# A one-core hybrid layer (gated DeltaNet and differential attention): load order and passes of the first projection, planned times of the gates' transpositions, weights of attention's order

## The chip, the cores and the metric

The kernel runs on one core of one Trainium2 chip. The metric is device microseconds of one execution; lower is better. The kernel before was run three times: median 1941.17 us (1939.21 to 1942.13).

## What is computed

One layer over 1024 latent tokens with a prefix of 256 context tokens, model width 1024. Modulation comes from c, normalisation and one wide projection feed two branches, and both are gated, merged and projected:

```python
shift, scale, gate = jnp.split(jax.nn.silu(c) @ w_ada + b_ada, 3, axis=-1)
h = rms_norm(x) * (1.0 + scale[:, None]) + shift[:, None]      # context: the same with c_ctx
qkv_a, z_a, a_raw, b_raw, q_b, k_b, v_b, z_b, gates = split_cols(h @ w_in)
o_a = gdn_bidirectional(...)   # 8 heads: short conv on q, k, v, then a chunked gated delta rule both ways
o_b = diff_attend(q, k, v, lam)  # 8 heads: softmax(s0) - lam * softmax(s1), times v
y_a = rms_norm(o_a) * silu(z_a);  y_b = rms_norm(o_b) * (1 - lambda_init) * silu(z_b)
merged = g_a * (y_a @ w_oa) + g_b * (y_b @ w_ob)
return x + gate * (merged @ w_out)
```

Wide products are computed in three passes from operands split in a high and a low part (high·high, low·high, high·low), so each product of the reference is three matmuls.

## The kernel before

**How the order comes about.** The program is written as streams: Python generators, each of which yields one operation after the other as an engine, an estimated duration, the tokens (planned ends) that it waits for, and the code that issues it. A planner, at build time, decides in which order the operations go to each engine. `turn_flow` (front and attention) finds the earliest planned start of all streams' next operations and, among those on that engine that could start within TOL = 0.02 us of it, takes the stream with the smallest bias; `flow` (convolution, DeltaNet and filling projections) takes the smallest sum of start and bias, and the projections that fill TensorE's waits there have FB0 added to their start. `later(t, us)` only moves a planned end: it delays nothing on the chip, but may put other operations first. At run time every engine goes through its list in order, and waits by semaphores.

**Stages** (times from the trace). The front, up to about 75 us: `loads` issues all transfers on SP's queue (L265 is the line of each of these DMAs); `modulation` multiplies a padded c with w_ada in four parts u, each in two halves of 1 MB (TensorE mp<-wa,pad, sixteen matmuls of 256 columns; the sums are copied to mrow by VectorE, L354, and ScalarE, L352); `rms` squares each block of 128 tokens of x on ScalarE (L381), takes the power -0.5 on POOL and scales on VectorE (L385); `turns` transposes scaled x (pt); `turned` makes h, its high part on ScalarE (L402), the whole on VectorE (L405) and the low part (L408) on VectorE for even k and POOL for odd k; `weights` splits the first weights of w_in (wr) in wh (ScalarE, L316) and wl (VectorE, L317). `main` is the first projection (mm<-hs,wh and mm<-hs,wl). Tokens go in groups: 0 and 1 of four latent blocks each (512 columns), 2 of the two context blocks. ORDER runs over the four units u of k pairs and the groups 0 and 1, then group 2.

The convolution stage follows (to about 430 us), in which the gates of the DeltaNet are computed once: three matmuls into one bank (gp), a copy to gcc (VectorE, L848), a difference (L849), exponentials (egl on ScalarE, L850), and ten transpositions of gcc in groups of four, four and two (trg), copied to gr (VectorE, L861). The three banks `tr0` to `tr2` go round through the list `pfree`, in which each comes with the tokens of its last readers.

Then the DeltaNet scan with filling projections (to about 1300 us; their last outputs are SiLU gates zo, ScalarE, L1039), attention (to about 1760 us), and the second half of the merge with the output projection (to the end).

**Attention** has named streams whose biases are the table ABIAS, to each of which `due` adds the index of the tile in work, so that a difference of 10 between two weights is a lead of ten tiles: scores (TensorE s<-kk,qh and s<-kk,ql), evs (VectorE takes s out of its bank, L1565), softs (the minimum, then the exponential over 1280 keys on ScalarE, L1578), scales (L1595 on ScalarE, or POOL), adds (POOL, L1602), turns (TensorE t<-ct,S, ten transpositions of one tile of weights, three banks), highs (ScalarE cast ah<-t, L1634), lows (VectorE al, L1639), att_out (TensorE v<-ah and v<-al, 30 matmuls for two tiles), outs (ScalarE's square osq, L1669, and through gateq VectorE's oT, L1676), sums (TensorE v<-ct,osq, columns of sums), norms (a power, the transposition m<-ct,bry), merge (TensorE ma<-y,wh and ma<-y,wl, the first half of the merge, which fills waits) and mouts (VectorE g, L1812, empties the merge's bank). There are 64 tiles of scores: 8 heads of 8 blocks. merge and m share one bank, pm.

Of the kernel before, what the change touches and what calls it, by code (L numbers as in the profile page):

```python
# [17 lines left out]
P = 128  # L18
D = 1024
KT = D // P  # L20
# [14 lines left out]
PE, DVE, ACT, POOL, DMA, ADMA, DV2, PL1 = range(8)  # L35
# [8 lines left out]
class Block:  # L44
# [30 lines left out]
    def flow(self, until):  # L75
# [3 lines left out]
        while not until():  # L79
# [3 lines left out]
            for s in self.streams:  # L83
# [7 lines left out]
                if s[1] is None:  # L91
                    start += self.FB0 if self.units_done < self.FT else self.FB1
                if h[0] == PE and len(h) > 4 and self.heat - self.HEAT * (start - clk[PE]) < 0:
# [144 lines left out]
    def front(self, st, early, kv0):  # L238
# [5 lines left out]
        xt, wa, raws, T = {}, {}, {}, {}  # L244
# [19 lines left out]
        def get(us, dst, src, deps=()):  # L264
            return DMA, us, list(deps), lambda: nc.sync.dma_start(dst, src)  # L265

        def loads():
            r = [(yield get(0.02, rows[0:8, :], a["c"].rearrange("o (k p) -> (o k) p", p=P))),
                 (yield get(0.02, rows[8:16, :], a["c_ctx"].rearrange("(k p) -> k p", p=P)))]
            T["rows"] = [self.later(x, -1.2) for x in r]  # L270
            for o in "xw0sy123zv":
                if o == "s":
                    r = [(yield get(0.05, rw2[0:24, :], a["b_ada"].rearrange("o (k p) -> (o k) p", p=P))),
                         (yield get(0.02, rw2[24:25, :], a["gdn_norm_w"])), (yield get(0.02, rw2[25:26, :], a["diff_norm_w"])),
                         (yield get(0.25, rw3, a["conv_w"].rearrange("o j (k p) -> (o j k) p", p=P)))]
                    T["rw"] = r
                elif o in "0123":
                    u = int(o)
                    if u == 3:
                        yield lambda: ("mm", 0) in T  # L280
                    for i in range(2):
                        if u == 2:
                            wa[u, i] = fu.tile([P, KT, W], F32, tag=f"u{i}", name="wa")
                        elif u == 1:
                            wa[u, i] = self.hc.tile([P, KT, W], F32, tag=f"s2{i}", name="wa")
                        else:
                            wa[u, i] = self.wab[0].tile([P, KT, W], F32, tag=("wh", "wl")[i], name="wa")
                        T["wa", u, i] = self.later((yield get(3.0, wa[u, i], a["w_ada"][0, :, i * D + u * W:i * D + (u + 1) * W].rearrange(
                            "(k p) n -> p k n", p=P), [T["mm", 0]] if u == 3 else ())), -1.2)
                elif o == "w":  # L290
                    for s in range(2):
                        k = slice(s * KT // 2, (s + 1) * KT // 2)
                        raws[s] = raw = self.wr.tile([P, KT // 2, W], F32, tag="wr", name="wr")
                        T["w0", s] = self.later((yield get(1.5, raw, kv0.rearrange("(k p) n -> p k n", p=P)[:, k])), -1.2)
                elif o == "v":
                    yield lambda: ("w", 1) in T and ("mm", 3) in T
                    for s in range(2):
                        k = slice(s * KT // 2, (s + 1) * KT // 2)
                        raws[s] = raw = self.wr.tile([P, KT // 2, W], F32, tag="wr", name="wr")
                        yield get(1.5, raw, self.wcols(C_VB).rearrange("(k p) n -> p k n", p=P)[:, k], [T["w", s]])  # L300
                        T["w1", s] = self.later((yield get(0.3, grw[:, k], a["w_in"][0, :, C_AB:C_AB + 32].rearrange(
                            "(k p) n -> p k n", p=P)[:, k])), -1.2)
                else:
                    for t in groups["xyz".index(o)]:
                        T["x", t] = self.later((yield get(1.5, xt[t], a["x"][0, t * P:(t + 1) * P, :] if t < NL else
                                                          a["ctx"][0, (t - NL) * P:(t - NL + 1) * P, :])), -1.2)

        def weights():
            for i, n in ((0, W), (1, W + 32)):
                yield lambda: (f"w{i}", 1) in T  # L310
                hl, ends = [self.wab[1 - i].tile([P, KT, n], F32R, tag=t, name=t) for t in ("wh", "wl")], []
                for s in range(2):
                    k = slice(s * KT // 2, (s + 1) * KT // 2)
                    for o, rw, us in ((0, raws[s], 0.256), (W, grw[:, k], 0.032))[:1 + i]:
                        c = slice(o, o + rw.shape[2])
                        t1 = yield ACT, 0.1 + 3.6 * us, [T[f"w{i}", s], T.get(("mm", 3))], lambda: nc.scalar.copy(hl[0][:, k, c], rw)  # L316
                        t2 = yield DV2, 4.7 * us, [t1], lambda: V.tensor_tensor(  # L317
                            hl[1][:, k, c], rw, hl[0][:, k, c].bitcast(F32), ALU.subtract)
                        ends += [t1, t2]
                    self.raw_t[s] = t2  # L320
                    if i == 0:
                        T["w", s] = [t1, t2]
                T["hl"] = T.get("hl", hl)
                if i:
                    self.parts_[1] = *hl, ends

# [85 lines left out]
        def main():  # L412
            pts = [self.pm.tile([P, 512], F32, tag="mm", name="mm") for _ in range(5)]
            for g, ks in ORDER:
                n = len(groups[g]) * P
                for s, k in [(s, k) for s in range(2) for k in ks]:
                    yield lambda: ("h", g, k) in T and ("w", k // 4) in T
                    th, tl, _ = self.hsel(groups[g][0])
                    pt = pts[4][:, s * W:s * W + W] if g == 2 else pts[2 * s + g]
                    for i, (wt, ht) in enumerate(((0, th), (0, tl), (1, th))):  # L420
                        e = yield PE, 0.2265 if n == 512 else 0.1195, [T["h", g, k], T["w", k // 4]], lambda: self.mm(
                            pt, T["hl"][wt][:, k, s * P:(s + 1) * P], ht[:, k, :n], k == i == 0, k == KT - 1 and i == 2)
                    if k == KT - 1:
                        self.first_[s, g] = pt, e
            self.parts_done, self.part_t[0] = 1, e

# [378 lines left out]
    def gates(self):  # L805
# [12 lines left out]
        te = yield DMA, 0.1, [], lambda: nc.sync.dma_start(ea, a["a_log"].rearrange("o d h -> o (d h)").to_broadcast([P, NS]))  # L818
        x, y, s, z, w = (big[:, i] for i in range(5))
# [5 lines left out]
        te = yield ACT, 0.2, [te], lambda: nc.scalar.activation(ea, ea, AF.Exp), AF.Exp  # L825
# [16 lines left out]
        ib, bank, gp = self.bank("gp")  # L842
# [5 lines left out]
        tg = yield DVE, 0.25, [t], lambda: V.tensor_copy(self.gcc, v(0))  # L848
        t1 = yield DVE, 0.25, [t, tg], lambda: V.tensor_tensor(z, v(NT * NS), self.gcc, ALU.subtract)  # L849
        te = yield ACT, 0.3, [t], lambda: nc.scalar.activation(self.egl, v(NT * NS), AF.Exp), AF.Exp  # L850
        self.pfree.append((ib, [t1, te]))
        td = yield ACT, 0.3, [t1], lambda: nc.scalar.activation(self.edk, z, AF.Exp), AF.Exp
        yield ACT, 0.3, [tg], lambda: nc.scalar.activation(self.eg, self.gcc, AF.Exp), AF.Exp
        gr = gs.tile([P, LT], F32, tag="gtmp", name="gr")[:NS]
        for b0 in range(0, NT, 4):
            nb = min(4, NT - b0)
            yield lambda: self.pfree
            ib, bank, pt = self.bank("trg")
            for t in range(nb):
                e = yield PE, 0.109, [self.later(tg, 3.0), bank], lambda: self.tr(pt[:NS, t * P:(t + 1) * P], self.gcc[:, b0 + t])  # L860
            e = yield DVE, 0.6, [e, td], lambda: V.tensor_copy(gr[:, b0 * P:(b0 + nb) * P], pt[:NS, :nb * P])  # L861
            self.pfree.append((ib, e))
        yield DMA, 0.2, [e], lambda: nc.sync.dma_start(self.gcd.rearrange("d h n -> (d h) n"), gr)


# [570 lines left out]
    def named(self, n, gen):  # L1436
        s = self.entry[n] = [gen, self.ABIAS.get(n, 0), None, None]
        s[2] = next(gen, None)
        self.streams.append(s)

    def due(self, n, i):

        self.entry[n][1] = self.ABIAS.get(n, 0) + self.DUE * i

# [38 lines left out]
    WB = -0.17  # L1483
    FT = 38
    LEFT = 3
    FB0 = 0.05
    FB1 = 0.36
    COLD = 0.4
    HEAT = 0.55
# [245 lines left out]
    def side_start(self):  # L1735
# [10 lines left out]
    ONACT = (1, 2, 3)  # L1746
    TOL = 0.02
    PACE = 4.48
    ABIAS = dict(rels=-0.59, softs=8.84, norms=5.82, gateq=-27.29, sums=-18.71,
                 outs=-21.73, lows=-2.4, highs=-9.33, adds=36.19, scales=31.0, evs=22.29, mouts=-3.31,  # L1750
                 att_out=1.9, turns=3.19, scores=-21.22, merge=25.46)
    KEEP = 3

    def side_values(self):
# [454 lines left out]
```

## Time and profile before

| | us |
|---|---|
| median of three runs | 1941.17 |
| the profiled execution | 1941.8 |
| its span | 1939.9 |
| VectorE busy | 1453.6 |
| ScalarE busy | 1063.6 |
| POOL busy | 679.6 |

The page of the profile gives busy times by engine, a strip of the span in slices, the chain that ended last, and groups of instructions by line. PE is TensorE, PEld its weight loads, DVE VectorE, ACT ScalarE, POOL GpSimd, SP the queue that issues most DMAs. In a row of the timeline stand start, duration, engine, line, operation, output and inputs with their sizes, and the count of instructions; in brackets the idle time of the engine just before it, and what ended that. A group's row has the same idle time summed. Matmuls overlap, so their durations are longer than their distance from start to start.

### The profile page before, as it was taken

Reading aid. Unit: us, or ns where it says so; the run is one execution under the profiler, and the core shown is the slowest. Engines: PE = TensorE matmul, PEld = TensorE weight load, DVE = VectorE, ACT = ScalarE, POOL = GpSimd, SP = SyncE. Lnnn points to the kernel's source line nnn. Section 1 sums busy time; section 2 is a strip of 40 time slices with the busy share of each in tenths; the row PEclk is TensorE's granted clock in tenths of the full one; section 3 lists DMA queues with packets and bytes.
Section 4 is the critical chain, followed back from the end, with each engine's and each line's share of the span. In section 5 each row is a group of like instructions: output and inputs, shape, how many; then the busy total and the mean of one; then the engine's idle time right before and its main releaser. Section 6 shows DMA issues by size and latency. Waiting matters only on the chain.

```text
span 1939.9 us, 37460 instructions
## 1 busy us (share of the span) xinstructions
PE 1901.0 (98%) x13807; PEld 1675.0 (86%) x13807; DVE 1453.6 (75%) x3613; ACT 1063.6 (55%) x2189; POOL 679.6 (35%) x610
## 2 busy tenths in 40 slices
PE   6999999999999999999999999999999999999999
PEld 4978888899999998888888888887997888888887
DVE  4687998957887888767864965337996979985577
ACT  4543444426233563677575655448885868883222
POOL 3200000005541342343433232326766657671203
PEclk9999999999999999999999999999999999999999
DMA  9144535574545557667686565665436474226542
GB/s 333 61 133 98 138 95 134 127 194 171 173 141 184 173 188 230 232 196 236 196 291 199 183 199 166 206 236 201 129 123 205 162 244 148 83 88 221 185 148 87
DMA packets 383038, 336.39 MB, mean 173 GB/s; under 512 B 142609, under 2 KB 323443, under 8 KB 381831
## 3 DMA queue, kind: packets, MB, share of 16 engines
q1 hardware_dynamic: 382855, 333.99, 54.9%
q8 instruction: 109, 1.79, 0.4%
q14 instruction: 74, 0.61, 0.1%
HBM read 222.14 MB, written 111.79 MB: 172 GB/s over the span
## 4 chain that ended last, share of the span: by engine, by line
PE 83%; DVE 6%; DMA 4%; ACT 3%; issue 2%; POOL 1%; SPq 1%; DVEq 0%; ACTq 0%; POOLq 0%
PE mm L56 42%; PE s L56 6%; PE v L56 5%; PE chain L56 5%; PE mb L56 5%; PE ma L56 4%; PE x L56 3%; PE t L63 3%; PE out L56 3%; PE gram L56 1%; DVE S L1565 1%; DVE ac L595 1%; PE tr L63 1%; PE pz L56 1%; PE mp L56 1%
## 5 line engine op out<-in xcount | busy, mean ns | idle before, releaser
L56 PE MATMUL mm<-hs,wh 128*128 128x512 f32 (+1 forms) x2048 | 648.2, 390 | 1.5 <-DVE hs L408 1.4
L56 PEld LDWEIGHTS mm<-hs,wh 128*128 128x128 f32 x2048 | 371.1, 189 | 58.7 <-DVE hs L408 2.0
L56 PE MATMUL mm<-hs,wl 128*128 128x512 f32 (+1 forms) x1024 | 397.3, 388 | 1.0 <-POOL wl L886 1.0
L56 PE MATMUL mm<-wh,hs 128*128 128x256 f32 (+1 forms) x1792 | 332.8, 286 | 0.2 <-ACT sq L978 0.2
L56 PEld LDWEIGHTS mm<-wh,hs 128*128 128x128 f32 x1792 | 280.8, 191 | 0.7 <-ACT sq L978 0.4
L1565 DVE TENSOR_SCALAR_CACHE_REDUCE S<-s,rsq 128x512 f32<-128x512 f32 (+1 forms) x384 | 239.6, 655 | 30.8 <-PE s L56 28.1
L56 PE MATMUL mm<-wl,hs 128*128 128x256 f32 (+1 forms) x896 | 255.7, 285 | 0.0
L1602 POOL TENSOR_TENSOR S<-S 128x1280 f32<-128x1280 f32 x64 | 189.0, 2956 | 92.2 <-ACT S L1595 91.0
L56 PEld LDWEIGHTS mm<-hs,wl 128*128 128x128 f32 x1024 | 193.7, 189 | 29.7 <-POOL wl L886 1.4
L1578 ACT ACTIVATE S<-S,mn 128x1280 f32<-128x1280 f32 x128 | 175.2, 1371 | 51.2 <-DVE mn L1577 50.7
L56 PEld LDWEIGHTS mm<-wl,hs 128*128 128x128 f32 x896 | 171.3, 191 | 0.1
L595 DVE SCALAR_TENSOR_TENSOR ac<-xc,convT,ac 128x1284 f32<-128x1284 f32 (+1 forms) x96 | 138.7, 1447 | 11.3 <-ACT ac L593 10.7
L56 PE MATMUL s<-kk,qh 128*128 128x512 f32 (+1 forms) x384 | 143.1, 373 | 1.6 <-DVE S L1565 1.4
L56 PE MATMUL s<-kk,ql 128*128 128x512 f32 (+1 forms) x384 | 133.5, 359 | 0.0
L1639 DVE TENSOR_TENSOR al<-t,ah 128x512 fp32r<-128x512 f32 (+1 forms) x192 | 106.8, 594 | 7.4 <-ACT ah L1634 6.1
L580 POOL MEMSET xc<- 128x2 f32 (+1 forms) x64 | 3.6, 100 | 299.8 <-ACT sq L629 113.6
L1160 DVE TENSOR_TENSOR ts<-ts,tmp 80x31 f32<-80x31 f32 (+15 forms) x248 | 94.0, 379 | 6.0
L1158 DVE TENSOR_TENSOR tmp<-ab,ts 80x31 f32<-80x31 f32 (+15 forms) x248 | 93.1, 375 | 6.8 <-DMA ab<-da 1.4
L1323 ACT ACTIVATE vd<-chain,edk 128x128 f32<-128x128 f32 x144 | 52.3, 371 | 78.0 <-PE chain L56 72.2
L56 PE MATMUL ma<-y,wh 128*128 128x512 f32 x256 | 93.1, 410 | 1.7 <-DVE g L1812 1.7
L1634 ACT CAST ah<-t 128x512 fp32r<-128x512 f32 (+1 forms) x192 | 88.1, 521 | 9.8 <-PE t L63 8.5
L56 PE MATMUL v<-al,vh 128*128 128x256 f32 x320 | 90.6, 283 | 0.7 <-DVE al L1639 0.7
(296 smaller groups left out, 4314.0 us busy)
## 6 DMA issues: line engine op xcount, KB each, us to landing
wr<-in_w_in_dram SPq DMA_DIRECT2D x48, 512.0 KB, 6.3
hx<-in_w_in_dram SPq DMA_DIRECT2D x64, 256.0 KB, 4.6
x<-xq SPq DMA_DIRECT2D x64, 256.0 KB, 5.0
X<-gcd SPq DMA_DIRECT2D x8, 1280.0 KB, 7.6
kd<-col SPq DMA_DIRECT2D x40, 256.0 KB, 2.2
xq<-X SPq DMA_DIRECT2D x16, 640.0 KB, 8.8
kk<-kd SPq DMA_DIRECT2D x16, 640.0 KB, 6.1
kq<-gkq SPq DMA_DIRECT2D x8, 1152.0 KB
```

The costliest lines, as they stand in the source:

```text
L56: self.nc.tensor.matmul(out, lhsT, rhs, start=start, stop=stop)
L63: self.nc.tensor.transpose(out, src, self.ident[:src.shape[0], :src.shape[0]])
L580: x["e"].append((yield PL1, 0.1, [old], lambda: nc.gpsimd.memset(xc[:, a:b], 0.0)))
L595: t = yield DV2, 1.21e-3 * wd, [t], lambda: nc.vector.scalar_tensor_tensor(ac[:, :wd], xc[:, j:j + wd], self.convw(j, x["ct"]), ac[:, :wd] ...
L1158: t = yield DV2, n * w / 960.0 + 0.08, [t if j else self.later(t, 2.5), t1], lambda: V.tensor_tensor(tv, ab[:, j + 1:, j:j + 1].to_broadca ...
L1160: t = yield DV2, n * w / 960.0 + 0.08, [t, t1], lambda: V.tensor_tensor(ts[:, j + 1:, :w], ts[:, j + 1:, :w], tv, ALU.subtract)
L1323: td = yield ACT, 0.251, [t], lambda: nc.scalar.activation(vd, pc[:, 1], AF.Copy, scale=self.edk[:, c, g:g + 1])
L1565: e = yield DVE, 0.675 if m == 512 else 0.408, [e, self.sfree[c].get(n - 4 + c)], lambda: self.nc.vector.tensor_scalar(x["S"][c][:, o:o + ...
L1578: x["x"].append((yield ACT, 1.36, [e], lambda: nc.scalar.activation(S, S, AF.Exp, bias=x["mn"][:, c:c + 1], scale=-1.0, accum_out=w["l0"][ ...
L1602: e = yield POOL, 2.9, [e], lambda: self.nc.gpsimd.tensor_tensor(S0, S0, S1, ALU.add)
L1634: e = yield ACT, 0.48 if nb == 4 else 0.27, [t, y["old", k]], lambda: self.nc.scalar.copy(y["ah", k][:, :, q], pv)
L1639: t = yield DVE, 0.603 if k < 2 else 0.322, [e, y["old", k]], lambda: self.nc.vector.tensor_tensor(y["al", k][:, :, q], pv, y["ah", k][:, ...
```

## The change

It has four parts. In `loads`, the order of groups goes from `xw0sy123zv` to `0sxwy123zv`: the first part of w_ada and the small rows go to the queue ahead of the first group of x and the first weights. In `main`, groups 0 and 1 are multiplied in two sweeps over (s, k): first the high part of h with wh and wl, then the low part with wh; each waits only for the half of h and of the weights that it reads. (`T["hl"]` is set earlier for that; for group 2 the sweeps are within each s.) In the gates, the planned ends of the readers of gp's bank are moved by 2.5 us and those of trg's banks by 2.0. And FB0 and five weights of ABIAS are other numbers.

```diff
-            for o in "xw0sy123zv":
+            for o in "0sxwy123zv":
...
-                for s, k in [(s, k) for s in range(2) for k in ks]:
+                for w, s, k in sorted(((w, s, k) for w in range(2) for s in range(2) for k in ks), key=lambda x: x[g // 2]):
...
-                    for i, (wt, ht) in enumerate(((0, th), (0, tl), (1, th))):
-                        e = yield PE, 0.2265 if n == 512 else 0.1195, [T["h", g, k], T["w", k // 4]], lambda: self.mm(
-                            pt, T["hl"][wt][:, k, s * P:(s + 1) * P], ht[:, k, :n], k == i == 0, k == KT - 1 and i == 2)
-                    if k == KT - 1:
+                    for i, (wt, ht) in enumerate(((0, tl),) if w else ((0, th), (1, th))):
+                        e = yield PE, 0.2265 if n == 512 else 0.1195, [T["h", g, k][w], T["w", k // 4][wt]], lambda: self.mm(
+                            pt, T["hl"][wt][:, k, s * P:(s + 1) * P], ht[:, k, :n], k == i == w == 0, k == KT - 1 and w == 1)
+                    if k == KT - 1 and w:
...
-        self.pfree.append((ib, [t1, te]))
+        self.pfree.append((ib, [self.later(t1, 2.5), self.later(te, 2.5)]))
...
-            self.pfree.append((ib, e))
+            self.pfree.append((ib, self.later(e, 2.0)))
...
-    FB0 = 0.05
+    FB0 = 0.07
...
-    ABIAS = dict(rels=-0.59, softs=8.84, norms=5.82, gateq=-27.29, sums=-18.71,
-                 outs=-21.73, lows=-2.4, highs=-9.33, adds=36.19, scales=31.0, evs=22.29, mouts=-3.31,
-                 att_out=1.9, turns=3.19, scores=-21.22, merge=25.46)
+    ABIAS = dict(rels=-0.59, softs=8.84, norms=5.82, gateq=-27.29, sums=-14.02,
+                 outs=-21.73, lows=-2.4, highs=12.49, adds=25.06, scales=31.0, evs=22.29, mouts=-3.31,
+                 att_out=-3.07, turns=3.19, scores=-20.84, merge=25.46)
```

What stands on the engines now differs at three places. The first is ScalarE's list at the start of the program: sil is the SiLU of c, junk,ss the squares of x (one row for each run of blocks), mrow the modulation's sums, hs the high parts of h. Before:

```order
L330 ACTIVATE sil<-rows 16x128
L381 ACTIVATE junk,ss<-x 128x1024 x4
L316 CAST wh<-wr 128x1024 x2
L352 COPY mrow<-mp 128x256
L381 ACTIVATE junk,ss<-x 128x1024 x2
L402 ACTIVATE hs<-pt,mods 128x512 x2
L381 ACTIVATE junk,ss<-x 128x1024 x2
L402 ACTIVATE hs<-pt,mods 128x512 x2
```

and of the change:

```order
L330 ACTIVATE sil<-rows 16x128
L352 COPY mrow<-mp 128x256
L381 ACTIVATE junk,ss<-x 128x1024 x4
L317 CAST wh<-wr 128x1024 x2
L402 ACTIVATE hs<-pt,mods 128x512 x2
L381 ACTIVATE junk,ss<-x 128x1024 x4
L402 ACTIVATE hs<-pt,mods 128x512 x2
```

The copy of the first modulation's sums moved ahead of the four squares and the two casts of weights, and the second group's four squares now stand together behind the first two high parts.

The second place is TensorE's list where the gates' transpositions stand among the projections of the convolution stage. Before:

```order
L56 MATMUL mm<-hs,wl 128x512
L63 MATMUL trg<-ct,gcc 16x128 x4
L56 MATMUL mm<-hs,wh 128x512 x2
L56 MATMUL mm<-hs,wl 128x512
L56 MATMUL mm<-hs,wh 128x512 x2
L56 MATMUL mm<-hs,wl 128x512
L56 MATMUL pq<-ks,fold 128x40
L56 MATMUL mm<-hs,wh 128x512 x2
L56 MATMUL mm<-hs,wl 128x512
L63 MATMUL trg<-ct,gcc 16x128 x4
```

and of the change:

```order
L56 MATMUL mm<-hs,wl 128x512
L63 MATMUL trg<-ct,gcc 16x128 x4
L56 MATMUL mm<-hs,wh 128x512 x2
L56 MATMUL mm<-hs,wl 128x512
L56 MATMUL mm<-hs,wh 128x512 x2
L63 MATMUL trg<-ct,gcc 16x128 x4
L56 MATMUL mm<-hs,wl 128x512
L56 MATMUL mm<-hs,wh 128x256 x2
L56 MATMUL mm<-hs,wl 128x256
```

The first four stand 22 projections behind the matmuls of gp instead of 21, the second four closer behind the first four (five projections instead of nine), and the last two, not shown, come some 25 projections later; since the three banks go round in another order, the first four write another bank than gp's and the second four write gp's.

The third place is TensorE's list in attention, around a transposition m of a head's root-mean-squares. Before, at the second head:

```order
L56 MATMUL ma<-y,wl 128x512
L56 MATMUL ma<-y,wh 128x512
L63 MATMUL t<-ct,S 128x128 x4
L56 MATMUL ma<-y,wh 128x512
L63 MATMUL t<-ct,S 128x128 x6
L56 MATMUL ma<-y,wl 128x512
L63 MATMUL m<-ct,bry 8x128
L56 MATMUL v<-ah,vh 128x256
```

and of the change, as at five of the eight heads:

```order
L56 MATMUL v<-al,vh 128x256
L56 MATMUL v<-ah,vl 128x256
L63 MATMUL m<-ct,bry 8x128
L63 MATMUL t<-ct,S 128x128 x10
L56 MATMUL s<-kk,qh 128x512
L56 MATMUL s<-kk,ql 128x512
L56 MATMUL s<-kk,qh 128x512
L56 MATMUL s<-kk,ql 128x512
L56 MATMUL s<-kk,qh 128x256
L56 MATMUL s<-kk,ql 128x256
L56 MATMUL v<-ct,osq 128x1 x2
L56 MATMUL ma<-y,wh 128x512 x2
```

The transposition m stood straight behind a matmul of ma, whose bank it takes over; now a whole block of v matmuls stands between them, and the order around it is the same from head to head.

## What is predicted

> **What bounds the kernel now.** I read the busy times first, then the busy time of each engine by stretch, then the groups of TensorE's instructions by shape with the idle time ahead of each, and last the timeline at the places that the change touches.
>
> ```profile
> PE 1901.0 (98%) x13807; PEld 1675.0 (86%) x13807; DVE 1453.6 (75%) x3613; ACT 1063.6 (55%) x2189; POOL 679.6 (35%) x610
> ```
>
> TensorE is busy 98% of 1939.9 us. The change leaves the number and the shapes of its matmuls and transpositions as they are, so TensorE's work is the same in both kernels and only the time in which it waits, or runs at half pace, can be won or lost. The stretches (columns: span, busy time of PE, PEld, DVE, ACT and POOL, granted clock, DMA share, GB/s) say where that time lies:
>
> ```profile
> 20.00:30.00 10.00, 8.48 (x43) 4.74 (x36) 6.11 (x10) 6.20 (x11) 5.85 (x9) 1.00 1.07 389
> 30.00:40.00 10.00, 10.00 (x94) 6.92 (x94) 6.43 (x11) 4.27 (x6) 2.92 (x3) 1.00 1.09 374
> 1300.00:1350.00 50.00, 46.30 (x249) 38.36 (x248) 37.73 (x132) 38.35 (x56) 24.71 (x10) 0.97 0.62 220
> 1350.00:1400.00 50.00, 49.86 (x338) 44.84 (x337) 46.54 (x160) 42.66 (x73) 35.87 (x17) 1.00 0.44 148
> 1450.00:1500.00 50.00, 47.69 (x283) 40.20 (x282) 31.55 (x102) 30.21 (x52) 27.66 (x17) 1.00 0.61 205
> ```
>
> Up to 30 us TensorE waits for the loads and the normalisation (8.48 of 10 us busy, much of it at half pace, as a row below shows); from 30 on it is full, so whatever is won there stays won until the next wait that does not move with it. The passage from projections to attention (1300 to 1350) leaves 3.7 us, the stretch at 1450 another 2.3. By groups (out<-in and count, busy time and mean ns, idle time ahead with what ended it):
>
> ```profile
> L56 PE MATMUL s<-kk,qh 128*128 128x512 f32 x256 | 106.6, 416 | 1.4 <-DVE S L1565 1.2
> L56 PE MATMUL ma<-y,wh 128*128 128x512 f32 x256 | 93.1, 410 | 1.7 <-DVE g L1812 1.7
> L56 PE MATMUL v<-al,vh 128*128 128x256 f32 x320 | 90.6, 283 | 0.7 <-DVE al L1639 0.7
> L63 PE MATMUL t<-ct,S 128*128 128x128 f32 x640 | 87.0, 275 | 2.8 <-ACT zo L1039 1.9 <-DVE al L1639 0.8
> L56 PE MATMUL v<-ct,osq 128*128 128x1 f32 x128 | 17.8, 243 | 1.0 <-DVE oT L1676 0.5
> L63 PE MATMUL m<-ct,bry 128*8 128x128 f32 x8 | 2.2, 270 | 0.8 <-DVE g L1812 0.8
> L63 PE MATMUL trg<-ct,gcc 128*16 128x128 f32 x10 | 1.6, 273 | 3.0 <-ACT egl L850 2.1 <-DVE gr L861 0.9
> ```
>
> These seven rows hold 11.4 us, small items of known cause. The sum is made from them and from the front, against the profiled execution's 1941.8 us, which is 0.6 above the median of the three runs, 1941.17.
>
> **Front: load order and passes.**
>
> ```profile
> 9.87 1.06 ACT L381 ACTIVATE junk<-x 128x1024 bf16<-128x1024 f32 x1
> 15.33 1.93 PE L56 MATMUL mp<-wa,pad 128*32 128x256 f32 x16 [9.89 <-DMA wa<-in_w_ada_dram]
> 20.75 0.37 ACT L352 COPY mrow<-mp 128x256 f32<-128x256 f32 x1 [7.25 <-PE mp L56]
> 24.07 0.79 PE L56 MATMUL mm<-hs,wh 128*128 128x512 f32 x1
> 26.31 0.79 PE L56 MATMUL mm<-hs,wh 128*128 128x512 f32 x1 [1.45 <-DVE hs L408]
> 25.74 1.66 POOL L408 TENSOR_TENSOR hs<-hf,hs 128x512 fp32r<-128x512 f32 x1 [1.09 <-DVE hf L405]
> 30.25 0.75 DVE L385 TENSOR_SCALAR x<-x,xry 128x1024 f32<-128x1024 f32 x1 [0.77 <-POOL xry L179]
> 31.20 0.39 PE L56 MATMUL mm<-hs,wl 128*128 128x512 f32 x1
> ```
>
> The transfers run one behind the other at some 390 GB/s (389 in the row of 20 to 30), 2.7 us for 1 MB. Ahead of w_ada's first part stand 3 MB today, and it lands at 15.3. With those 3 MB behind it, it lands 8 us earlier, at 7.3 (second half 9.9), and the four blocks of x at 11.4, 12.8, 14.1 and 15.5, the two halves of w_in at 16.9 and 18.2. What comes later in the queue keeps its place.
>
> ScalarE now copies mrow (0.37) ahead of the four squares; at a pitch of 1.2 us the last of them ends at 17.7. The power on POOL and VectorE's scaling (the row at 30.25 begins 0.77 after its root and takes 0.75) bring x to 19.4; two casts of w_in, 1.05 us each, end by then, and the first hs follows. The first mm stands at about 20.7 against 24.07. By the new order of passes it needs only the high half, so the 1.45 us at 26.31 (a wait for the low half on VectorE) goes as well.
>
> What is late next is the second group of x, whose landing does not move. Its four squares stand behind two hs activations, as two of them do now; the last ends near 26 and POOL's low half (1.66 us) lies beside. The last scaling of that group ends at 31.0 now (30.25+0.75) and by this chain at 29.7: **−1.3**. In addition all twelve mm of the first unit can be done by then, where nine were by 31.2 (the first at 24.07, the ninth in the last row): three times 0.23 (the pitch at full pace, from two matmuls in 0.45 us between 137.90 and 138.35 in a fence below), 0.7 us, of which I count half, since they stand where TensorE has otherwise little to do. I take **−1.6**; the ends are −2.3 (everything counts) and 0 (next paragraph).
>
> ```profile
> 27.89 1.94 PE L56 MATMUL mp<-wa,pad 128*32 128x256 f32 x16
> 32.46 1.07 PE L56 MATMUL mp<-wa,pad 128*32 128x256 f32 x16
> ```
>
> The granted clock reads 1.00 in all stretches of the front, yet the same sixteen matmuls took 1.94 us at 27.89 and 1.07 at 32.46: TensorE ran at half pace until near 30. After the change its first burst, 20.7 to about 26, ends earlier than the second group of x is scaled, and between 26 and 28 to 29.7 it has little to do. If the fast pace comes with the first burst and is lost in that hole, up to 1.7 us of the front is spent again, which takes the whole term; that is a rival below. The Trainium skill (TensorE: Matmul & The Clock Gate, section on the two states of the clock gate) says that half rate is the default, that full rate needs about 3.4 us of sustained work and that an idle window of that length takes it back. The trace agrees on the factor of two, with 1.94 against 1.07; by that rule the hole here is just short of a window or as long as one.
>
> **Gates' transpositions.**
>
> ```profile
> 132.58 0.32 DVE L838 SCALAR_TENSOR_TENSOR gtmp<-gtmp,ea 128x160 f32<-128x160 f32 x1
> 137.90 0.61 PE L56 MATMUL mm<-hs,wh 128*128 128x512 f32 x2
> 138.35 0.39 PE L56 MATMUL mm<-hs,wl 128*128 128x512 f32 x1
> 138.70 0.32 DVE L848 COPY gcc<-gp 128x160 f32<-128x160 f32 x1
> 140.48 0.30 ACT L850 ACTIVATE egl<-gp 128x160 f32<-128x160 f32 x1 [0.44 <-DVE gtmp L849]
> 140.84 0.60 PE L63 MATMUL trg<-ct,gcc 128*16 128x128 f32 x4 [2.10 <-ACT egl L850]
> 144.61 0.60 PE L63 MATMUL trg<-ct,gcc 128*16 128x128 f32 x4 [0.86 <-DVE gr L861]
> ```
>
> The first four transpositions reuse the bank from which ACT still reads egl, the second four the bank that VectorE empties into gr: 2.10+0.86, 3.0 us of idle. In the new order the first four take another bank and wait for gcc alone, which comes out 1.8 us ahead of egl. Yet they stand only one matmul later (0.23 us), and VectorE's queue from L838 to L848, 6.1 us by these rows, has 0.75 us more put into it. So some 1.1 us is left there. The second four, five matmuls on, now wait for egl: 0.2. The last two, behind some 25 matmuls, wait for nothing. 3.0−1.3: **−1.7**, ends 0 and −3.0.
>
> **Projections to attention.**
>
> ```profile
> 1321.10 0.39 PE L56 MATMUL mm<-hs,wl 128*128 128x512 f32 x1
> 1321.37 1.28 ACT L1039 ACT_TABLE_LOAD   x1
> 1322.66 1.08 ACT L1039 ACTIVATE zo<-mm 128x512 f32<-128x512 f32 x2
> 1323.40 2.19 PE L63 MATMUL t<-ct,S 128*128 128x128 f32 x10 [1.92 <-ACT zo L1039]
> ```
>
> TensorE's first transposition after the last projection waits 1.92 us for a bank that zo empties, and zo stands behind an exponential and a table load of 1.28 us. In the new order the last scores lie some 42 matmuls ahead of the last projection instead of a dozen, so exponential and load are over by then, and only zo (0.6 and a signal) is left: **−1.1**, ends 0 and −1.9. ScalarE has four more table loads in this stretch, 5.1 us of it; it is busy 38 of 50 us there, so I cost them at nothing; with that cover gone one of them costs TensorE up to 1.28.
>
> **Attention.**
>
> ```profile
> 1339.60 0.48 PE L56 MATMUL s<-kk,qh 128*128 128x512 f32 x1
> 1340.45 0.60 PE L56 MATMUL v<-ct,osq 128*128 128x1 f32 x4 [0.37 <-DVE oT L1676]
> 1457.43 0.48 PE L56 MATMUL ma<-y,wl 128*128 128x512 f32 x1
> 1458.70 0.27 PE L63 MATMUL m<-ct,bry 128*8 128x128 f32 x1 [0.79 <-DVE g L1812]
> ```
>
> The merge has one bank. At 1458.70 the transposition m comes straight behind the last ma (0.23 us of work), while VectorE first has to multiply the bank by the gate g. That is the 1.7 and 0.8 us of the groups, 2.5 in all. The new order puts 1.1 us of TensorE's work or more between such neighbours nearly everywhere, 30 v matmuls (3.5 us) mostly ahead of m. All but the last goes: **−2.2**, ends 0 and −2.5.
>
> The column sums v<-osq wait for ScalarE's square and VectorE's oT. Start to start the wait at 1340.45 is 0.85 us where 0.23 is the pitch, so 0.62 lost where the idle column says 0.37; the group's 1.0 us is then about 1.7. Between the last v and its sums lie 1.5 us of work now and 2.4 to 3.5 in the new order: **−1.5**, ends 0 and −1.7.
>
> The rest of the new weights reshuffles who waits for whom, with the same work. Reuse distances of the score banks grow (median 2.7 to 3.1 us), those of the transposition banks grow in the median (4.6 to 5.8) and shrink at the least (2.1 to 1.2). The rows for s, t and v<-al above hold 2.9 us without zo: I take 0, ends −2.9 and +2.9. FB0 leaves the distances of the scan's chain as they were: 0, ends ±1.5, about the idle time of its largest rows.
>
> Sum: −1.6−1.7−1.1−2.2−1.5 = −8.1, so 1933.7 beside the profiled 1941.8, and **1933.0** beside the median.
>
> **The rivals.** A measurement of this kernel tells about 0.2% (3.9 us) from no change: faster is below 1937.3, slower above 1945.1.
>
> *The front gives nothing*, the clock falling back in the hole: the sum without 1.6, 1934.7. For it speaks that TensorE idles longer there than now, against it that the hole has transpositions and the second part of the modulation in it. 0.12.
>
> *The gates' edit does not do what it says*: one matmul later is hardly later, and with 0.75 us more ahead of gcc the 3.0 us may stay: 1934.8. 0.08.
>
> *The next operand is late.* At 1350 VectorE is busy 46.5 of 50 us: where TensorE no longer waits for g or osq, it waits for S or al. The attention terms (2.2+1.5) and the passage (1.1) come back, 1937.9, between 1937.3 and 1941. 0.17.
>
> *More is won*: the regular order takes the waits on s, t and v<-al too, 2.9 of them and their share between starts: 1929, down to 1926. 0.11.
>
> *Slower.*
>
> ```profile
> 1333.71 1.33 ACT L1634 CAST ah<-t 128x512 fp32r<-128x512 f32 x3
> 1334.92 1.38 ACT L1578 ACTIVATE S<-S,mn 128x1280 f32<-128x1280 f32 x1
> ```
>
> The weight of highs (12.49) now stands behind that of softs (8.84), so a ready exponential, 1.38 us, goes ahead of a cast that empties a transposition bank. There are three such banks, and al and the v matmuls follow the cast. If half of it shows on TensorE, a tile costs 0.7 us (estimate); among the 64 tiles of scores 12 such take the gain, and from 17 on, +12, the kernel is slower: 1945 to 1951. For it: the shortest reuse of those banks, 1.2 us, is below 1.38. Against it: the median is 5.8, and ACT is free 7 of 50 us at 1350. 0.15.
>
> **How the numbers follow.** The forecast as it stands, 1930 to 1936, has 0.37. With the front's and the gates' rivals and "more", faster has 0.37+0.12+0.08+0.11 = 0.68; same 0.17; slower 0.15. The range runs from 1926 (the end of "more") to 1942, past the end of the late operand, and leaves out most of the slower case and a little below, some 0.2.
>
> **What would show it.** First mm near 20.7, the mp of the second unit at 1.94 or 1.07 us, and the last scaling of the second group near 29.7. trg: idle 1.3 instead of 3.0, released by gcc and egl. First t after the projections: under 1 us, by zo. The groups ma and m: next to nothing by g L1812; osq under 0.3. If instead t<-ct,S or v<-al show waits by L1634 or L1639 of 5 us and more, the highs' weight has decided; if idle time by S L1565 has grown as the others fell, the next operand was late. The forecast is wrong if TensorE's idle time outside these rows grows.

## The result, and the profile after

The changed kernel takes 1948.35 us (median of nine runs, 1943.9 to 1953.1) against 1941.17 (nine runs): the ratio is 1.0037, 95% interval 1.0025 to 1.0049, some 7 us slower, where 8 us faster was forecast. The profiled execution was the longest of the nine, 1953.1 us with a span of 1951.3, so its sizes are read with a second profile of the same program beside it (change_again below, 1947.9). Busy times of the page:

```profile
PE 1908.2 (98%) x13807; PEld 1680.7 (86%) x13807; DVE 1458.4 (75%) x3613; ACT 1069.2 (55%) x2193; POOL 681.5 (35%) x610
```

The number of matmuls is the same. TensorE's groups that the prediction rested on, with three others:

```profile
L56 PE MATMUL s<-kk,qh 128*128 128x512 f32 x256 | 106.2, 415 | 0.5 <-DVE S L1565 0.4
L56 PE MATMUL ma<-y,wh 128*128 128x512 f32 x256 | 92.2, 411 | 0.0
L63 PE MATMUL t<-ct,S 128*128 128x128 f32 x640 | 85.0, 273 | 2.7 <-DVE al L1639 2.7
L56 PE MATMUL v<-ct,osq 128*128 128x1 f32 x128 | 16.8, 235 | 1.3 <-DVE oT L1676 1.3
L63 PE MATMUL m<-ct,bry 128*8 128x128 f32 x8 | 2.2, 271 | 2.2 <-POOL bry L179 2.2
L63 PE MATMUL trg<-ct,gcc 128*16 128x128 f32 x10 | 1.6, 272 | 0.0
L56 PE MATMUL chain<-r,x 128*128 128x128 f32 x288 | 53.4, 279 | 3.6 <-DVE r L1314 3.0 <-DMA x<-xq 0.5
L63 PE MATMUL tr<-ct,fin 128*128 128x128 f32 x144 | 22.2, 277 | 3.3 <-DVE X L1130 1.9 <-POOL fin L1008 0.6 <-DVE fin L1000 0.5
L56 PE MATMUL p<-Z,RR 32*32 32x32 f32 x640 | 10.3, 198 | 4.5 <-issue 4.5
```

The waits named in the prediction are mostly gone: trg 3.0 to 0, ma 1.7 to 0, the zo part of t 1.9 to 0, s 1.4 to 0.5. Two are not (the sums by oT 1.3, m by the power on POOL 2.2), and one has grown: t waits 2.7 us for VectorE's al instead of 0.8. The last three rows, all of the scan (products along its chain, transpositions, and products of 32 columns), have 11.4 us of idle time. In the kernel before they have 2.7:

```profile
L56 PE MATMUL chain<-r,x 128*128 128x128 f32 x288 | 51.3, 277 | 0.2 <-DVE r L1314 0.2
L63 PE MATMUL tr<-ct,fin 128*128 128x128 f32 x144 | 22.2, 276 | 1.5 <-DVE fin L1000 1.1 <-POOL fin L1008 0.2
L56 PE MATMUL p<-Z,RR 32*32 32x32 f32 x640 | 10.1, 198 | 1.0 <-issue 0.9
```

The other half does not stand in the idle column. The stretches of the changed kernel (columns as in the prediction: after DVE, ACT and POOL come the granted clock, the DMA share and GB/s); the first four follow one another, the others come in pairs:

```profile
24.60:28.00 3.40, 1.81 (x7) 0.89 (x6) 2.17 (x3) 2.33 (x5) 3.17 (x4) 1.00 1.09 386
28.00:31.40 3.40, 1.42 (x18) 0.69 (x18) 1.86 (x3) 0.00 (x0) 2.71 (x4) 1.00 1.09 366
31.50:34.80 3.30, 3.16 (x17) 2.33 (x13) 2.27 (x5) 1.55 (x2) 0.00 (x0) 0.50 1.09 362
34.90:38.20 3.30, 3.30 (x20) 1.75 (x21) 0.51 (x1) 0.37 (x1) 1.64 (x1) 0.50 1.09 381
659.50:662.90 3.40, 1.47 (x13) 1.29 (x12) 3.33 (x9) 0.00 (x0) 0.69 (x1) 1.00 0.00 0
663.00:666.30 3.30, 3.30 (x17) 3.30 (x16) 2.81 (x6) 0.59 (x1) 0.00 (x0) 0.50 0.52 174
1127.20:1130.50 3.30, 1.42 (x117) 1.08 (x116) 1.46 (x4) 2.42 (x9) 2.14 (x4) 1.00 1.03 263
1130.60:1133.90 3.30, 3.27 (x12) 2.63 (x12) 1.95 (x5) 2.79 (x10) 0.00 (x0) 0.50 1.20 307
1338.80:1342.10 3.30, 1.48 (x8) 0.63 (x6) 1.91 (x6) 1.72 (x4) 0.00 (x0) 1.00 1.01 304
1342.20:1345.50 3.30, 3.30 (x15) 3.11 (x15) 3.10 (x10) 0.12 (x1) 0.00 (x0) 0.50 1.03 288
```

A stretch in which TensorE is busy 1.4 to 1.5 of some 3.4 us is followed by one at half the granted clock, in which it is busy nearly all the time, at half the pace. (The very first stretch, with 1.81 us of busy time, is not; and the second stretch at half clock in the front follows one that was busy 3.16 of 3.30 us. A sixth half-clock stretch stands at 601.5.) The kernel before has one such place behind the front, the wait for zo:

```profile
1320.20:1323.60 3.40, 1.48 (x8) 0.97 (x7) 0.27 (x1) 3.37 (x5) 1.83 (x1) 1.00 0.00 0
1323.70:1327.00 3.30, 3.30 (x14) 3.01 (x13) 0.42 (x1) 2.45 (x5) 1.92 (x1) 0.50 0.73 250
```

To split the time by stage I subtract, from the time between two marks, the work of the matmuls between them at full pace (their number by shape times the usual distance from start to start: 0.227 us for 512 columns, 0.1195 for 256, and so on). What is left is time lost on TensorE, by waits and by half clock; the split is an estimate good to some tenths:

| lost on TensorE, us | before | change | change again |
|---|---|---|---|
| to the end of the front | 26.4 | 28.8 | 29.6 |
| convolution, to the scan's first product (gram) | 6.6 | 4.1 | 4.9 |
| scan and filling, to the first s | 32.3 | 46.3 | 41.0 |
| passage, to the first t | 2.2 | 0.6 | 0.2 |
| attention, to the last v | 20.9 | 17.0 | 15.8 |
| rest, to the last matmul | 1.9 | 3.7 | 3.8 |
| half-clock windows of 3.41 us behind 25 us | 1 | 6 | 5 |

So the convolution stage with the gates, the passage and attention won 8.0 us in the first profile and 8.8 in the second (1.8 and 1.9 of it lost again behind the last v), and the front and the scan lost 16.4 and 11.9. A further 1.2 us in each stands behind the last matmul (5.1 us to the end of the span, 3.9 before).

### The profile page after: what moved, and what is told of

Read it like the earlier page. It is cut to its first block, busy times and chain, and to the rows that moved or that the text cites. A ratio compares the mean times of both kernels' runs of the same rounds, so it can differ in the third digit from the quotient of the medians.

```text
span 1951.3 us, 37487 instructions
## 1 busy us (share of the span) xinstructions
PE 1908.2 (98%) x13807; PEld 1680.7 (86%) x13807; DVE 1458.4 (75%) x3613; ACT 1069.2 (55%) x2193; POOL 681.5 (35%) x610
## 4 chain that ended last, share of the span: by engine, by line
PE 59%; DVE 2%; DMA 2%; issue 1%; ACT 1%; POOL 1%; SPq 0%; POOLq 0%; DVEq 0%; ACTq 0%
PE mm L56 19%; PE s L56 7%; PE v L56 6%; PE chain L56 5%; PE mb L56 5%; PE ma L56 4%; PE x L56 3%; PE t L63 3%; PE out L56 3%; PE gram L56 1%; PE pz L56 1%; DVE S L1565 1%; PE z L56 1%; DMA sk<-gkq 0%; DMA xq<-qk 0%
## 5 line engine op out<-in xcount | busy, mean ns | idle before, releaser
L1634 ACT CAST ah<-t 128x512 fp32r<-128x512 f32 (+1 forms) x192 | 88.3, 516 | 13.6 <-PE t L63 10.4
L1287 POOL TENSOR_TENSOR x<-x,ct 128x256 f32<-128x256 f32 x64 | 50.8, 800 | 125.5 <-DMA x<-xq 66.3
L56 PE MATMUL ma<-y,wh 128*128 128x512 f32 x256 | 92.2, 411 | 0.0
```

Source lines behind the costliest of these rows:

```text
L56: self.nc.tensor.matmul(out, lhsT, rhs, start=start, stop=stop)
L1287: u["tqk"] = yield POOL, 0.72, [u["tx"]], lambda: nc.gpsimd.tensor_tensor(x[:, 1], x[:, 1], (self.up, self.lo)[d].unsqueeze(1).to_broadcas ...
L1634: e = yield ACT, 0.48 if nb == 4 else 0.27, [t, y["old", k]], lambda: self.nc.scalar.copy(y["ah", k][:, :, q], pv)
```

## The experiments

Each is the kernel before or the changed one with some of the parts altered, and compared with runs of the kernel before on the same chip (ratio, with its interval). Beside the time stands the mean granted clock of all runs of the kernel: one window of 3.41 us at half clock lowers it by 0.0009 (3.41 x 0.5 / 1941) and costs up to 1.7 us, all of it where TensorE is busy. For the kernel before it is 0.9995.

**front_alone**: the first two parts of the diff on the kernel before.

```diff
-            for o in "xw0sy123zv":
+            for o in "0sxwy123zv":
...
+                for w, s, k in sorted(((w, s, k) for w in range(2) for s in range(2) for k in ks), key=lambda x: x[g // 2]):
```

> The kernel before with the load order and the two passes alone; scan and attention keep their order. Theory (the hole behind the first burst costs granted clock): in the profiled run of the whole change two windows at half clock (6.8 us) stand at 31.4, and the front ends 2.3 us later (76.7 against 74.4); so 1943 to 1944.5, and nothing else lost. Rival (the front gives its 1.6 us and the loss comes from elsewhere): 1939.5. The number of half-clock windows behind the front stays as before (one, at the passage to attention).

Measured 1944.21 us, ratio 1.0019 (1.0009 to 1.0029), clock 0.9966. The theory's size holds: the clock stands for 3.3 windows. The expectation that the number of windows behind the front stays as before did not hold place by place: this profile has one at 151.5 in the convolution stage and none at the passage to attention. Three in the front follow one another:

```profile
20.00:28.60 8.60, 6.15 (x18) 4.09 (x18) 7.08 (x8) 6.04 (x10) 4.22 (x6) 1.00 1.06 393
28.60:38.80 10.20, 8.46 (x47) 4.67 (x48) 4.78 (x7) 1.93 (x3) 4.29 (x5) 0.50 1.09 369
```

(The trace's records of the clock begin at 25.2 us here, with the first change to the full clock; the 1.00 of the first row says nothing of the time ahead of that.)

**front_filled**: front_alone with matmuls of no use in the hole.

```diff
-                        e = yield PE, 0.109, [tb, T["xs", t]], lambda: self.tr(pt[:, j * P:(j + 1) * P], xt[t][:, k * P:(k + 1) * P])
+                        e = yield PE, 0.109, [tb, T["xs", t]], lambda: (
+                            self.tr(pt[:, j * P:(j + 1) * P], xt[t][:, k * P:(k + 1) * P]),
+                            [self.mm(T["pts"][4], T["hl"][0][:, 0, 0:P], self.hsel(0)[0][:, 0, :512])
+                             for _ in range(5 if (g, k) == (1, 0) and j < 3 else 0)])
```

> The load order and the passes as in front_alone, and in addition five matmuls without use behind each of the first three transpositions of the second group of x, where TensorE waits 1.0 to 1.2 us each (they write a bank that is started anew later; 15 x 0.23 = 3.4 us of work). Theory (the front loses by half-clock windows that the hole brings): no half-clock window between 25 and 40 us, the front ends 3 to 5 us earlier than in front_alone (77.7), so 1939 to 1941. Rival (the order of the front itself loses, the clock is a symptom): the added 3.4 us stand on the path or change nothing: 1944 to 1947.

Measured 1942.23 us, ratio 1.0001 (0.9991 to 1.0011), clock 0.9995. 3.4 us more work, and by the ratios 3.5 us less time than front_alone; the time is 1 us above the theory's range. The same stretch, and the hole itself:

```profile
28.60:38.80 10.20, 10.11 (x80) 6.53 (x83) 4.47 (x8) 2.10 (x4) 3.88 (x5) 1.00 1.09 370
```

```profile
27.64 1.41 PE L56 MATMUL mm<-hs,wh 128*128 128x512 f32 x5
28.88 0.33 PE L63 MATMUL pt<-ct,x 128*128 128x128 f32 x1
28.96 1.38 PE L56 MATMUL mm<-hs,wh 128*128 128x512 f32 x5
...
31.84 1.07 PE L56 MATMUL mp<-wa,pad 128*32 128x256 f32 x16
```

The transpositions come when they came, and the sixteen matmuls of the modulation take 1.07 us; in front_alone, without the filling, they took 1.94 (at 31.22). That the front loses by the clock is shown.

**loads_alone** and **passes_alone**: one line of the front's two parts each (`"0sxwy123zv"` alone; the sorted loop with its waits by halves alone).

> The kernel before with the load order alone, each step still in three passes. Theory (the hole comes from the load order, as the first group is done before the second is scaled): half-clock windows after 25 us, 1943 to 1945. Rival (it needs the passes as well, since the wait for the low half keeps the first burst later): 1940 to 1941.

> The kernel before with the two passes alone. Theory: the first burst closes the 1.45 us wait for the low half, the full clock comes no later than at 30 us, and no hole opens, as x and w_ada land as before: 1939 to 1941. Rival (the passes themselves cost, by a second load of the same weights): slower by 1 us and more.

Measured 1942.4 us, ratio 1.0007 (0.9997 to 1.0016), clock 0.9992; and 1940.09 us, ratio 0.9990 (0.9981 to 0.9999), clock 0.9995. The load order alone comes to the full clock at 30.1 in its profile, as the kernel before does at 30.0, keeps it through the rest of the front, and wins nothing; its time lies between the theory and the rival. The passes alone win some 2 us (0.2 to 3.7 by the interval). The hole that costs the clock needs both, as the rival of loads_alone has it: with the two passes the first burst is over at 28.2, without them at 30.9, and the last block of x is scaled at 32.3 in both profiles.

**gates_alone**: the planned ends alone.

```diff
+        self.pfree.append((ib, [self.later(t1, 2.5), self.later(te, 2.5)]))
...
+            self.pfree.append((ib, self.later(e, 2.0)))
```

> The kernel before with the later planned ends of gp's and trg's banks alone. Theory: the wait for egl and gr goes (3.0 us idle in two rows of trg), the rest is as before: about 1938.5. Rival (the wait moves to gcc or to the projections behind): 1941.

Measured 1941.08 us, ratio 0.9999 (0.9991 to 1.0008). Of the 3.0 us of trg 1.8 are left, in one place, by a bank that VectorE reads for another purpose:

```profile
144.83 0.60 PE L63 MATMUL trg<-ct,gcc 128*16 128x128 f32 x4 [1.78 <-DVE rk L644]
```

A gain of 1.2 us is below what this comparison can tell; the time is the rival's, with a wait for rk where the rival named gcc or the projections.

**weights_alone**: the five numbers of ABIAS alone; **weights_highs_back**: the same with `highs=-9.33`.

> The kernel before with the five weights of attention alone; everything up to attention keeps its order. Theory (attention gains what the profiled run of the whole change shows, 3.9 us, and 1.6 at the passage, less 1.8 at its end): 1937 to 1938. Rival (the weights give back at the end of attention what they win in it, m waiting for the power on POOL): 1940 to 1942.

> As weights_alone, with the weight of highs back at -9.33. Theory (weights_alone wins some 3 us in attention, and gives them back by the wait for the cast L1634 at 1331.4, 1.3 us with a half-clock window behind it, and by m and the sums at the end, 2 us): the wait for L1634 goes and its window with it, so 1938 to 1939.5. Rival (the highs' weight is what made the gain): 1941 to 1944.

Measured 1940.76 us, ratio 0.9999 (0.9990 to 1.0008), and 1947.57 us, ratio 1.0035 (1.0023 to 1.0046). The rival of the first holds, and so does that of the second, with a size beyond both. In weights_alone attention loses 17.7 us (20.9 before), although a second half-clock window stands in it; 1.8 us come back behind the last v. Its waits, old and new:

```profile
L56 PE MATMUL ma<-y,wh 128*128 128x512 f32 x256 | 92.2, 412 | 0.1
L56 PE MATMUL v<-ah,vh 128*128 128x256 f32 x320 | 90.7, 283 | 1.3 <-ACT ah L1634 1.3
L63 PE MATMUL t<-ct,S 128*128 128x128 f32 x640 | 84.7, 273 | 3.0 <-ACT zo L1039 1.9 <-DVE al L1639 1.0
L56 PE MATMUL v<-ct,osq 128*128 128x1 f32 x128 | 16.6, 233 | 1.1 <-DVE oT L1676 1.1
L63 PE MATMUL m<-ct,bry 128*8 128x128 f32 x8 | 2.2, 271 | 2.2 <-POOL bry L179 2.2
```

The 1.3 us by the cast L1634 is my slower rival's mechanism (two exponentials go ahead of the casts), at one tile of 64. Put back to -9.33, the weight of highs takes that wait down to 0.2, and attention loses 27.0 us: beside the other four weights the 12.49 is no cost but a gain of 9 us there. Alone it was not tried.

**fb0_alone**, **fb0_06**, **fb0_10**: `FB0 = 0.07`, `0.06`, `0.10` on the kernel before.

> The kernel before with FB0 = 0.07 alone: scan and filling projections in another order, attention in another order by that. Theory (the loss of the whole change sits in the scan stage, 14 us in its profiled run, by idle spots of 1.6 us and more, each followed by a half-clock window of 3.4 us): slower, 1945 to 1953, with two or more such windows between 450 and 1300. Rival (the scan stage of the whole change lost by an order that only all parts together bring): within 2 us of 1941.

> The kernel before with FB0 = 0.06 alone. Theory V (the value itself costs: the later the filling projections are allowed, the more TensorE waits in the scan): between 0.05 and 0.07, 1943 to 1945, with 33 to 37 us lost in the scan. Theory C (any other value gives another order of the whole scan, and its waits fall anew each time): no relation to the value, anywhere between 1939 and 1950.

> The kernel before with FB0 = 0.10 alone. Theory V: clearly slower than with 0.07 (1947.6), 1952 or more, 45 us and more lost in the scan. Theory C: no relation to the value, 1939 to 1950.

Measured 1947.58 us, ratio 1.0037 (1.0024 to 1.0050), clock 0.9992; 1961.78, ratio 1.0105 (1.0091 to 1.0119); 1957.91, ratio 1.0087 (1.0073 to 1.0100). Theory V falls: 0.06 is worse than 0.07 and 0.10. C holds in so far as there is no relation to the value, but its bound of 1950 was too low. In the profile of fb0_alone the scan loses 37.0 us (32.3 before), and against its expectation no half-clock window stands in it. TensorE is idle there 3.1 us longer than before, by other waits, such as

```profile
880.90 0.68 PE L56 MATMUL chain<-S,sk 128*128 128x128 f32 x4 [1.70 <-DMA sk<-gkq]
```

With 0.06 the largest single loss stands at the passage: the first score goes to TensorE right behind the last projection, 7.7 us ahead of the load of its second operand, and what follows runs at half clock:

```profile
1321.95 0.40 PE L56 MATMUL s<-kk,qh 128*128 128x512 f32 x1
1330.01 0.77 PE L56 MATMUL s<-kk,ql 128*128 128x512 f32 x1 [7.67 <-DMA ql<-qd]
```

**change_fb0_back**: the whole change with `FB0 = 0.05`.

> The whole change with FB0 back at 0.05. Theory (the parts add up: front +3.7, gates and weights nothing, FB0 +7.0): 1944 to 1945, scan stage within 3 us of the 32 us that it loses before. Rival (the scan's loss comes from any new order, as the front and the gates alter what is left for it to fill with): 1947 to 1950, with 40 us and more lost in the scan.

Measured 1943.03 us, ratio 1.0008 (0.9998 to 1.0017), clock 0.9969. The scan loses 34.1 us, within the theory's 3 us, but the time lies 1 to 2 us below its sum. By the ratios FB0 in the whole change costs 5 to 6 us. The clock is as low as in front_alone, but the ratio is smaller (1.0008 against 1.0019), so the other parts seem to win back some of it.

**change_filled**: the whole change with the filling of front_filled. **change_again**: the changed program unaltered.

> The whole change with the fifteen matmuls without use in the front's hole; scan and attention keep the order of the change. Theory (the front's part of the loss is the clock, some 3 us, and the scan's part, 5 us and more, stays): 1944 to 1946.5, no half-clock window before 100 us, one to three of them in the scan in its profile. Rival (the later half-clock windows are a late effect of the front's, by its shift in time): 1940 to 1942, scan without them.

> The whole change once more, for a second profile of the same program. Theory (the waits of the scan belong to its order and come again at the same instructions, whether one is followed by a half-clock window depends on where the fixed 3.41 us windows fall): the waits for p<-Z,RR near 598 and 1128, for tr<-ct,fin near 660 and for chain<-r,x come again within some tenths of a us; the windows that follow may differ; 40 to 47 us lost in the scan. Rival (the profiled execution met a chance delay): about 35 us.

Measured 1946.31 us, ratio 1.0026 (1.0017 to 1.0036), clock 0.9976, no half-clock window before 100 us and two in the scan of its profile; and 1947.9 us. The scan loses 43.1 and 41.0 us. The waits come again at the same instructions, in change_again:

```profile
602.17 0.23 PE L56 MATMUL p<-Z,RR 32*32 32x32 f32 x1 [1.61 <-issue]
664.22 0.63 PE L63 MATMUL tr<-ct,fin 128*128 128x128 f32 x4 [1.93 <-DVE X L1130]
1126.81 0.22 PE L56 MATMUL p<-Z,RR 32*32 32x32 f32 x2 [1.54 <-issue]
```

In the first profile these were 1.62, 1.93 and 2.01 us, each followed by a half-clock window; here the second has none behind it. The waits belong to the order, the windows behind them also to the moment.

**passes_gates_weights**: the changed kernel with the old load order and FB0 at 0.05, so that the two parts that cost are left out.

> The kernel before with the two passes, the gates' planned ends and the five weights, without the load order and with FB0 at 0.05; the scan keeps its order. Theory (the parts add up: passes -1.9 by ratio 0.9990, gates and weights nothing): 1938.5 to 1940.5, faster than before by 0.05 to 0.15%. Rival (the gates' wait and the weights' gain add to it): 1936 to 1938.

Measured 1938.35 us, ratio 0.9982 (0.9973 to 0.9992): the fastest version found, faster than both kernels, though not told apart from passes_alone (0.9981 to 0.9999). The time lies on the border of theory and rival. Its profile has no half-clock window between the front and the end.

## Why the prediction was wrong

**FB0, forecast 0 with ends ±1.5: this step failed.** "FB0 leaves the distances of the scan's chain as they were" was read off the order, and the distances did not show the waits. Alone it costs 7.0 us, with other values up to 20, in the whole change 5 to 6. The new order of the scan waits longer for late operands and for TensorE's own issue. In the two profiles of the change r holds chain<-r,x up for 3.0 and 1.8 us (0.3 in change_fb0_back), and issue holds p<-Z,RR up for 4.5 and 3.9 (0.8); in fb0_alone it is the load of sk, 1.7 (0.8 before). In the change, half-clock windows follow some of these waits. (The 1.9 us by X ahead of tr is not FB0's: change_fb0_back has it too, 1.8.) The ends that the runs would have asked for are 0 to 20 us, not 1.5.

**The front, forecast −1.6: +3.7 alone.** Three errors. The chain behind x runs at 1.5 us a block, by POOL and VectorE, not at ScalarE's 1.2, as the kernel before had shown (28.72 to 30.25). Rows of the changed kernel:

```profile
17.94 0.75 DVE L385 TENSOR_SCALAR x<-x,xry 128x1024 f32<-128x1024 f32 x1 [0.77 <-POOL xry L179]
19.46 0.75 DVE L385 TENSOR_SCALAR x<-x,xry 128x1024 f32<-128x1024 f32 x1 [0.77 <-POOL xry L179]
...
31.02 0.75 DVE L385 TENSOR_SCALAR x<-x,xry 128x1024 f32<-128x1024 f32 x1 [0.77 <-POOL xry L179]
```

So the first mm came at 21.6 instead of 20.7, and the second group's last scaling ended at 31.8, later than before (31.0), not at 29.7. The wait for a low half, 1.45 us before, did not go but passed to POOL's half:

```profile
26.71 0.96 PE L56 MATMUL mm<-hs,wh 128*128 128x512 f32 x3 [1.37 <-POOL hs L408]
```

And the rival "the clock falls back in the hole" was right in its mechanism and had 0.12; its price of 1.7 us was that of one window, where the front has two or three. The rule of the Trainium skill weighed there (TensorE: Matmul & The Clock Gate, the two states of the gate) is that an idle window takes the full rate back; the traces agree with it, except that about half a window of idle time is enough (last section).

**Gates, forecast −1.7**: in the whole change trg waits 0 and 0.4 us in the two profiles, where 1.3 were forecast to stay; the stage wins 1.7 to 2.5. Right there, though alone, with another order behind it, 1.8 us stay.

**Passage, forecast −1.1**: −1.6 and −2.0. The whole wait went, where 0.8 us of zo was to stay. No part alone does it: the wait is 1.9 us in weights_alone, 2.1 in fb0_alone and 1.9 in change_fb0_back. It went only with the order of the whole change. Before, a half-clock window stood behind this wait (the 0.97 of the stretch from 1300 to 1350), which the forecast gave no price.

**Attention, forecast −3.7**: −3.9 and −5.1 to the last v, then 1.8 and 1.9 lost behind it. The wait for g went as said. The sums did not gain in idle time (1.0 to 1.3 us), while s won 0.9; t waits 1.9 us more for al, and m 2.2 us for POOL instead of 0.8 for VectorE. By the idle column alone these rows hold no less than before (6.9 us against 6.7). What was won stands in busy time: t 87.0 to 85.0, the sums 17.8 to 16.8, ma 93.1 to 92.2, part of it the half-clock window of the kernel before. So the agreement in size is in part luck; the rival of the late operand was right about al, and the weights alone change nothing in the time.

**The slower rival** named highs. weights_highs_back shows the opposite: with the old weight of highs the time is longer (1.0035 against 0.9999).

## What to carry to other kernels

In these traces a wait on TensorE of more than 1.7 us costs itself and, where it falls within one window, up to 1.7 us again (from 1.2 us on now and then): price a hole by both, and ask of each hole that a gain opens whether it is that long. Where a planner's number reorders a whole stage, its effect had no size here that could be read off the order; bound it by what the stage's waits could be, or leave that number alone and take the local edits (here 0.9982 without it, 1.0037 with it). Of an edit in two halves, test the halves: the passes won alone, and lost with the loads.

## What the runs showed of the hardware

I had not expected how regular the clock's windows are. In all sixteen traces every change of the granted clock lies on a grid of 3.413 us, whose origin differs from run to run. Counted from 45 us on, 8820 windows at full clock: in 18 of them TensorE was idle for more than 1.72 us, about half, and all 18 were followed by a window at half clock (six of them hold the same wait, that of t for zo); between 1.15 and 1.72 us 7 of 39 were; below that none of 8763. This also explains by trace why one wait costs differently: the 2.10 us of trg before (138.7 to 140.8) lay across a border of the grid, 1.66 us in one window, and no half clock followed, while loads_alone's 1.96 in one window was followed by it.

Idle time does not explain every half-clock window. Behind 45 us, 25 half-clock windows in which TensorE was idle for less than 0.2 us were all followed by the full clock. In the front of three traces (both of the change, and front_alone) such a window, with at most 0.14 us of idle time, was followed by another half-clock window. Why the front stays at half clock for so long was not tried and stays open; that it does not fall there without the hole, front_filled shows.

The 640 matmuls p<-Z,RR of 32 columns start about 10 ns apart and then TensorE waits for nothing that the profile shows but its own issue: 0.9 us in the kernel before, 4.5 and 3.9 in the two profiles of the change. What makes that longer with one order than with another was not tried and stays open.
